# Mixing stage of a hybrid decoder layer: v with tokens on partitions, state products next to the first probabilities, SSM weights in room of their own, SSM outputs in token order

## The chip, the cores and the metric

The kernel runs on one core of a Trainium2 chip. The metric is the device time of one execution in microseconds (us); smaller is better. One execution was also recorded by the hardware profiler, which gives start and end of every instruction of TensorE (PE), its weight loads (PEld), VectorE (DVE), ScalarE (ACT), GpSimd (POOL) and of the DMA queues (SP issues nearly all transfers here).

## What is computed

One decoder layer over 512 tokens of width 1024: a first SwiGLU FFN, a mixing sub-layer, a second SwiGLU FFN, each between RMS norms, all in float32. The change is in the mixing sub-layer:

```python
h = rms_norm(x, mix_pre_g)
q, k, v, u = split(h @ w_mix_in, 4)              # four times 512 columns
attn = dilated_attention(q, k, v)                # 8 heads of 64; 3 dilations merged
ssm  = s5_mixer(u, ...)                          # 32 groups of 16 channels, 64 complex states
mixed = concatenate([attn, ssm], -1) @ w_mix_out
x = x + rms_norm(mixed, mix_post_g)
# s5_mixer: states by a linear recurrence over time; y = Re(C states) + d*u;
#           y = gelu(y); y * sigmoid(y @ w_glu + b_glu)
```

## The kernel before

**Number format.** Big products are made from three fp32r products each (high by high, high by low, low by high; `mm3`). So every weight tile is loaded raw (`load`, L99), cast to its high part on ACT (L93) and split off to its low part on DVE or POOL (L95). Raw tiles rotate through 3 buffers, the high and low parts through 4 each. Small products (scores, values, states, SSM outputs, transposes) are plain fp32; each fp32 product shows as two records.

**Layout.** Everything is held transposed: channels on partitions, the 512 tokens along the row. `mix` (from L835) runs in this order. Four u projections come ready from the boundary before. u is written to memory and read back in chunk order (a chunk is T = 4 tokens; 128 chunks, `U`). `proj` (from L844) makes a 128-channel piece of q, k or v: 24 products of 128x512, cut in two halves of 12 by a `yield`, and a DVE eviction (L856, L858) that also scales by the norm. A generator `pieces` lists the pieces; `f()` does the next half. v comes out with channels on partitions, and `turn_v` transposes it on PE (4 transposes for each head pair, L890) and copies it on ACT (L892).

**Attention.** For each of four head pairs: `attn_scores` (16 products; DVE adds the bias and takes the minimum, L793; ACT exponentiates, L795; the scaling by the sums is on DVE for pairs 0 and 1, on POOL and ACT for 2 and 3), `attn_turn` (10 transposes for each head, ACT copies L822), `attn_values` (16 products), `split` into the high and low halves of `cat`.

**SSM.** `states` (from L898) makes chunk states for 4 of 16 groups; `scan` (from L1058) runs the recurrence on DVE alone (L1064): 15 steps over the chunks of a row, one that copies, 6 over the row ends, and 4 that add the carried states. `go()` does one step. `outputs` (from L907) makes 4 groups' outputs from `M` (products of the last 4 inputs) and the states in `Hs`; its weights `w2` come by a DMA (L910) into a raw weight buffer. The outputs stand in the order (token within chunk, chunk); gelu follows on ACT and DVE, `glu` the gate, and the halves of `so` are written back in token order (L1046).

**Output projection.** `out_attn(m)` is the attention half: 12 products for each of 8 output tiles, with weights of 256 KB for each m. The SSM half (`yt`) is done in `boundary`, with the tail weights `tw` that `load_tail` has put in the pool `bdm`, which is opened where the attention pool `att` (scores, probabilities, q, k, v, and the scan's temporaries) was closed.

**What sets the order.** PE products and transposes, the projections' evictions and the scan's steps are pinned: each goes behind what was written before it for its engine (`fix`). Softmax, splits and weight loads are not pinned; a scheduler places them at build time by when their inputs and buffers are ready. Each engine then runs its queue strictly in order. PSUM has 8 banks.

Of the kernel before, what the change touches and what calls it, by code (L numbers as in the profile page):

```python
# [17 lines left out]
P = 128  # L18
S = 512
# [21 lines left out]
class Layer:  # L41
# [62 lines left out]
    def tail_weights(self, pool):  # L104

        self.tw = [pool.tile([P, KD * NT * P], F32R, name="tw", tag=f"tw{i}", bufs=1) for i in range(2)]

    def load_tail(self, src, c, pool):
        sl = slice(c * 2 * NT * P, (c + 1) * 2 * NT * P)
        self.load(src[c], (2 * NT, P), [t[:, sl] for t in self.tw], pool)  # L110
# [146 lines left out]
    def boundary(self, y, tail, ipost, half, inext, chunks):  # L257
# [4 lines left out]
        tw = [t.rearrange("p (m k j) -> p m k j", k=NT, j=P) for t in self.tw]  # L262
# [11 lines left out]
        def product(h, m):  # L274
            if m % 2 == 0 or m == 7:
                bank[0] = self.bank("yt").rearrange("p (m t) -> p m t", m=2)
            b = bank[0][:, m % 2 if m < 6 else 0]
            for k in range(NT):
                th, tl = tail(k)
                self.mm3(b, tw[0][:, m, k], tw[1][:, m, k], th[:, hs[h]], tl[:, hs[h]], k == 0, k == NT - 1)  # L280
            return bank[0]
# [32 lines left out]
        for ks in (range(NT - 1), (NT - 1,)):  # L314
            for m in range(2):
                for k in ks:
                    th, tl = tail(k)
                    self.mm3(b2[m], tw[0][:, m, k], tw[1][:, m, k], th[:, hs[0]], tl[:, hs[0]], k == 0, k == NT - 1)
# [52 lines left out]
    def ffn(self, n, first, scope, params):  # L371
# [68 lines left out]
        for f in range(NF):  # L440
            if f >= nfirst:
                products(f)
            if f == lag:
                for i in range(lag):
                    hidden(i)
            if f >= lag:
                hidden(f)
            if last and f == 6:
                for _ in hook:
                    pass  # L450
                yk = self.ktiles("y")
                y = lambda b, d: yk(2 * b + d)
            if last and f in (6, 12, 18):
                outp_tokens(f // 6 - 1)
            if not last and f in (7, 14):
                outp(f // 7 - 1)
            if f == NF - NT:
                for _ in hook:
                    pass
                early.close()  # L460
                self.tail_weights(scope.enter_context(self.tc.tile_pool(name="bd" + n, bufs=1)))
            if f >= NF - NT:
                self.load_tail(w_tail, f - (NF - NT), f % 2 == 1)
# [22 lines left out]
    def finish(self, y, tail):  # L486
# [3 lines left out]
        tw = [t.rearrange("p (k d c) -> p k d c", k=NT, d=2) for t in self.tw]  # L490
# [4 lines left out]
        def product(b, d, k0=0, k1=NT):  # L495
            if k0 == 0:
                o[b, d] = self.bank("yt")
            ts = slice(b * P, (b + 1) * P)
            for k in range(k0, k1):
                th, tl = tail(k)  # L500
                self.mm3(o[b, d], th[:, ts], tl[:, ts], tw[0][:, k, d], tw[1][:, k, d], k == 0, k == NT - 1)
# [323 lines left out]
    def attn_values(self, po, pt, vn):  # L825

        for kb in range(4):
            for i in range(2):
                self.mm(po[i * E:i * E + E, kb * P:], lhsT=vn[:, kb, i * E:i * E + E], rhs=pt[i][kb],
                        start=kb == 0, stop=kb == 3)  # L830
# [4 lines left out]
    def mix(self, first, scope):  # L835
        early = scope.enter_context(ExitStack())
# [49 lines left out]
        def turn_v(hp):  # L886

            o = self.bank("vt")
            for b in range(4):
                self.fix(nc.tensor.transpose(o[:, b * P:(b + 1) * P], pr[8 + hp][:, b * P:(b + 1) * P], self.ident))  # L890
            vn[hp] = ap.tile([P, 4, P], F32, name="vn", tag="vn", bufs=2)
            nc.scalar.copy(out=vn[hp].rearrange("p b c -> p (b c)"), in_=o)  # L892


        Hs = self.b16("Hs").rearrange("p (q n) (b k) -> p q (n b) k", q=2, k=NCH)
        ends = ap.tile([P, 2, NP, SC], F32, name="ends", tag="ends", bufs=1)
# [34 lines left out]
        mo = {}  # L931

        def out_attn(m, ks=range(4)):

            if m not in mo:
                mo[m] = self.bank("mo"), self.load(a["wmoa"][m], (4, P))
            o, (wh, wl) = mo[m]
            for k in ks:
                self.mm3(o, wh[:, k], wl[:, k], cat[:, k], cat[:, 4 + k], k == 0, k == 3)
# [9 lines left out]
        vn = {}  # L949
# [3 lines left out]
        def values(hp, pt):  # L953
            po = self.bank("pv")
            self.attn_values(po, pt, vn[hp])
            self.split(cat[:, hp], cat[:, 4 + hp], po)

        f()
        sc = scores(0)
        f(3)  # L960
        pt = [turn(sc[0])]
        f()
        pt.append(turn(sc[1]))
        f()
        sc = scores(1)
        states(0)
        states(4)
        turn_v(0)
        states(8)
        states(12)  # L970
        cat = self.b16("cat", F32R)
        scan = self.scan(ap, Hs, ends)
# [5 lines left out]
        def fg(n=1):  # L978
            for _ in range(n):
                f()  # L980
                go()

        values(0, pt)
        go(2)
        pt = [turn(sc[0])]
        fg()
        pt.append(turn(sc[1]))
        fg(5)
        for hp in (2, 3):
            sc = scores(hp)  # L990
            fg()
            turn_v(hp - 1)
            fg()
            values(hp - 1, pt)
            if hp == 2:
                go()
                pt = [turn(sc[0])]
                fg()
                pt.append(turn(sc[1]))
                fg(3)  # L1000
        go(7)
        pt = [turn(sc[0]), turn(sc[1])]
        y = self.ktiles("ymix")
        out_attn(0, range(3))
        go()
        turn_v(3)
        out_attn(1, range(3))
        values(3, pt)
        go()
        out_attn(2, range(3))  # L1010
        early.close()
        bdm = scope.enter_context(self.tc.tile_pool(name="bdm", bufs=1))
        self.tail_weights(bdm)
        zg = bdm.tile([P, 4, S], F32, name="zg")
        zt = self.b16("zz", F32R)
        tail = lambda c: self.load_tail(a["wmot"], c, False)
        for m in range(3):
            out_attn(m, (3,))
        go()
        out_attn(3)  # L1020
        for n4 in range(4):
            outputs(n4)
            if n4 < 3:
                if n4 == 0:
                    go()
                out_attn(4 + n4)
                tail(n4)
# [7 lines left out]
        def glu(m, ks=range(4)):  # L1035
# [4 lines left out]
            if 3 in ks:  # L1040
# [7 lines left out]
        for m in range(2):  # L1048
            glu(m, range(3))
        for m in range(2):  # L1050
            glu(m, (3,))
        glu(2)
        tail(3)
        glu(3)
        out_attn(7)
        return y, lambda i: (so[0][:, i], so[1][:, i])

    def scan(self, ap, Hs, ends):  # L1058
# [11 lines left out]
        def tmp(shape):  # L1070
            t = ap.tile([P, nb * (SI - 1) * SC], F32, name="sx", tag="scan", bufs=3)
# [26 lines left out]
        for n in range(0, NP, nb):  # L1098
# [12 lines left out]
            yield  # L1111
# [20 lines left out]
def pack(i):  # L1132
# [23 lines left out]
    o["wmi"] = mt(wm).reshape(16, P, D)  # L1156
    wo, o["wmot"] = two(mt(i["w_mix_out"][0]))
    o["wmoa"] = wo.reshape(KD, P, 4 * P)
# [34 lines left out]
```

## Time and profile before

| | us |
|---|---|
| median of 3 runs | 980.96 (978.39 to 981.84) |
| profiled execution, its time | 978.9 |
| its span, first to last instruction | 977.1 |
| PE busy | 948.4 |
| DVE, ACT, POOL busy | 532.9, 372.3, 223.5 |
| stage "mix" in the span | about 400 to 575 |

The time is the span and 1.8 us around it. The profile's page gives totals; for a stage of 175 us the useful views are the busy time in a stretch, the list of who waited for whom on PE, and the timeline of one engine, in which the idle time before an instruction and what ended it stand in brackets. A start-to-start distance in a timeline is what an instruction costs its engine; the duration printed beside it is longer, because the end of one overlaps the start of the next.

### The profile page before, as it was taken

The numbers are of one execution on the slowest core, as the hardware profiler recorded it, in microseconds if no ns is written. First come the engines' busy times: TensorE is split into PE (matmuls) and PEld (weight loads), VectorE is DVE, ScalarE is ACT, GpSimd is POOL, SyncE is SP. The second block draws the span as 40 slices with busy tenths as digits, with TensorE's granted clock in tenths as the row PEclk, the third lists the DMA queues.
The fourth block names the chain that finished last, engine by engine and source line by source line (L and its number), as shares of the span: only waits on it lengthen the run. The fifth ranks groups of instructions, "written<-read, shape, count | busy, mean of one in ns | idle before, by whom it ended". The sixth has DMA issues, their size and how long they took to land.

```text
span 977.1 us, 12902 instructions
## 1 busy us (share of the span) xinstructions
PE 948.4 (97%) x5088; PEld 792.6 (81%) x5088; DVE 532.9 (55%) x938; ACT 372.3 (38%) x616; POOL 223.5 (23%) x134
## 2 busy tenths in 40 slices
PE   9999999999999999999999699999999999999996
PEld 7888888888888899878667589888888888888884
DVE  7997214553265447658769567564225433444426
ACT  7353334431233234356553654443333222323312
POOL 2322212322233134300000024422122212222300
PEclk9999999999999999999999999999999999999998
DMA  8223334343343230473111530222223222333202
GB/s 261 91 103 113 103 119 150 100 166 103 108 131 116 76 130 23 118 211 120 54 51 50 185 126 23 92 95 93 89 87 108 101 93 87 108 98 131 95 0 87
DMA packets 38606, 102.48 MB, mean 105 GB/s; under 512 B 7665, under 2 KB 10737, under 8 KB 38001
## 3 DMA queue, kind: packets, MB, share of 16 engines
q1 hardware_dynamic: 37680, 98.50, 31.6%
q10 hardware_dynamic: 864, 3.15, 0.9%
q8 instruction: 40, 0.66, 0.3%
q14 instruction: 22, 0.17, 0.1%
HBM read 94.03 MB, written 7.60 MB: 104 GB/s over the span
## 4 chain that ended last, share of the span: by engine, by line
PE 86%; DVE 7%; ACT 3%; DMA 2%; issue 1%; POOL 0%; DVEq 0%; POOLq 0%; ACTq 0%
PE gu L121 46%; PE yo L121 20%; PE prj L121 6%; PE yt L121 5%; PE first L121 4%; PE st L121 1%; DVE sx L1064 1%; DVE Hs L1064 1%; DVE xl L144 1%; DMA wraw<-wmot 1%; DVE x L303 1%; PE pt L820 1%; ACT sc L795 1%; DMA w<-w2d 1%; PE idle L121 1%
## 5 line engine op out<-in xcount | busy, mean ns | idle before, releaser
L93 ACT CAST whi<-wraw 128x1024 fp32r<-128x1024 f32 (+5 forms) x161 | 155.8, 971 | 323.8 <-PE gu L121 126.9
L95 POOL TENSOR_TENSOR wlo<-wraw,whi 128x1024 fp32r<-128x1024 f32 (+2 forms) x62 | 156.3, 2521 | 525.9 <-ACT whi L93 525.9
L121 PE MATMUL gu<-xh,whi 128*128 128x512 f32 x656 | 257.6, 393 | 0.0
L121 PE MATMUL gu<-xh,wlo 128*128 128x512 f32 x656 | 255.6, 390 | 0.0
L121 PE MATMUL gu<-xl,whi 128*128 128x512 f32 x656 | 255.3, 389 | 0.0
L95 DVE TENSOR_TENSOR wlo<-wraw,whi 128x1024 fp32r<-128x1024 f32 (+5 forms) x99 | 111.6, 1130 | 124.9 <-ACT whi L93 124.5
L121 PEld LDWEIGHTS gu<-xh,wlo 128*128 128x128 f32 x656 | 123.1, 188 | 25.9
L121 PEld LDWEIGHTS gu<-xl,whi 128*128 128x128 f32 x656 | 123.2, 188 | 25.1
L121 PEld LDWEIGHTS gu<-xh,whi 128*128 128x128 f32 x656 | 123.2, 188 | 25.1 <-issue 0.4
L405 DVE TENSOR_TENSOR ut<-gu,rs 128x512 f32<-128x512 f32 x41 | 28.3, 689 | 104.0 <-PE gu L121 103.8
L141 DVE TENSOR_TENSOR al<-ut,ah 128x512 fp32r<-128x512 f32 x44 | 69.0, 1570 | 24.9 <-ACT ah L140 24.8
L121 PE MATMUL yo<-ah,whi 128*128 128x512 f32 x144 | 56.0, 389 | 0.0
L121 PE MATMUL yo<-al,whi 128*128 128x512 f32 x144 | 56.0, 389 | 0.0
L121 PE MATMUL yo<-ah,wlo 128*128 128x512 f32 x144 | 56.0, 389 | 0.0
L121 PE MATMUL yo<-whi,ah 128*128 128x512 f32 x144 | 56.0, 389 | 0.0
L121 PE MATMUL yo<-wlo,ah 128*128 128x512 f32 x144 | 56.0, 389 | 0.0
L121 PE MATMUL yo<-whi,al 128*128 128x512 f32 x144 | 56.0, 389 | 0.0
L403 DVE TENSOR_TENSOR gt<-gu,rs 128x512 f32<-128x512 f32 x41 | 28.2, 688 | 50.7 <-PE gu L121 50.6
L140 ACT CAST ah<-ut 128x512 fp32r<-128x512 f32 x44 | 27.2, 621 | 58.3 <-DVE ut L406 58.2
L121 PE MATMUL first<-xl,whi 128*128 128x256 f32 (+1 forms) x144 | 43.3, 300 | 2.2 <-DVE xl L144 2.2
L121 PE MATMUL first<-xh,whi 128*128 128x256 f32 (+1 forms) x144 | 43.9, 305 | 0.9 <-ACT xh L143 0.9
L406 DVE TENSOR_TENSOR ut<-ut,gt 128x512 f32<-128x512 f32 x44 | 40.7, 927 | 3.7
(192 smaller groups left out, 1426.9 us busy)
## 6 DMA issues: line engine op xcount, KB each, us to landing
wraw<-w2i SPq DMA_DIRECT2D x44, 512.0 KB, 3.5
wraw<-w1i SPq DMA_DIRECT2D x42, 512.0 KB, 3.5
wraw<-w2o SPq DMA_DIRECT2D x18, 512.0 KB, 3.5
wraw<-wmi SPq DMA_DIRECT2D x16, 512.0 KB, 3.5
wraw<-w1o SPq DMA_DIRECT2D x16, 448.0 KB, 3.4
x<-xT SPq DMA_DIRECT2D x8, 256.0 KB, 4.5
w1d<-w1s SPq DMA_DIRECT2D x8, 256.0 KB, 2.9
w2d<-zb SPq DMA_DIRECT2D x2, 1024.0 KB, 4.9
```

Of the source, the lines that this page charges most:

```text
L93: fix(self.nc.scalar.copy(out=hi, in_=raw))
L95: fix(eng.tensor_tensor(out=lo, in0=raw, in1=hi.bitcast(F32), op=ALU.subtract))
L121: i = self.nc.tensor.matmul(*a, **k)
L140: nc.scalar.copy(out=hi, in_=src)
L141: nc.vector.tensor_tensor(out=lo, in0=src, in1=hi.bitcast(F32), op=ALU.subtract)
L144: fix(nc.vector.scalar_tensor_tensor(out=lo, in0=src, scalar=scale, in1=hi.bitcast(F32), op0=ALU.mult, op1=ALU.subtract))
L303: fix(nc.vector.tensor_tensor(out=xk, in0=t, in1=xk, op=ALU.add))
L403: nc.vector.tensor_tensor(out=gt, in0=o[f][0], in1=r, op=ALU.mult)
L405: nc.vector.tensor_tensor(out=ut, in0=o[f][1], in1=r, op=ALU.mult)
L406: nc.vector.tensor_tensor(out=ut, in0=ut, in1=gt, op=ALU.mult)
L795: nc.scalar.activation(out=so, in_=so, func=AF.Exp, bias=nm[:, t:t + 1], scale=-1.0, accum_out=den[:, t:t + 1])
L1064: tt = lambda o, x, y, op: self.fix(V.tensor_tensor(out=o, in0=x, in1=y, op=op))
```

## The change

v is projected with tokens on partitions (`proj_v`: x is the stationary side, 512 columns of weights the moving side, evicted by ACT with the norm as a scale per partition), so `turn_v` goes. Both heads of pair 0 are turned and all `states` are made right after the first scores; all of v follows, in two pieces of 48 products. The scan has a pool of its own and starts its steps with v's pieces; its last four steps are cut in eight. `fg(i, ...)` does, for each i, `f()` and then `go(i)`. The low half of `cat` is pinned behind a step of the scan. `out_attn` takes its weights for two m at a time (512 KB) and is split up finer. The four `w2` loads get tiles in `bdm` (in the room that the last tail weights take later) and are issued together when `att` is closed. The four `outputs` come back to back and write PSUM with a stride, so that they stand in token order; `so` is then written straight. Tail weights are eight tiles in place of two.

```diff
-            t = pr[c] = ap.tile([P, S], F32, name="qkvT"[c // 4] + "T", tag="qk", bufs=5)
+            t = pr[c] = ap.tile([P, S], F32, name="qkT"[c // 4] + "T", tag="qk", bufs=4)
...
+        def proj_v(b0):
+            o = [self.bank("prv") for _ in range(2)]
+            for k in range(KD):
+                wh, wl = wv[k // 2]
+                for b in range(2):
+                    ts = slice((b0 + b) * P, (b0 + b + 1) * P)
+                    self.mm3(o[b], xh(k)[:, ts], xl(k)[:, ts], wh[:, k % 2], wl[:, k % 2], k == 0, k == KD - 1)
+                if k % 2:
+                    if k == KD - 1:
+                        for b in range(2):
+                            nc.scalar.activation(out=vn[:, b0 + b], in_=o[b], func=AF.Copy,
+                                                 scale=r4[:, b0 + b:b0 + b + 1])
+                    yield
...
-            w2 = self.wp.tile([P, 2, 4, P], F32, name="w2", tag="wraw", bufs=3)
-            nc.sync.dma_start(out=w2, in_=self.w2d[:, :, 4 * n4:4 * n4 + 4])
+            w2 = w2s[n4]
             b = self.bank("ys")
+            bt = b.rearrange("p (s i t) -> p t i s", s=SC, t=T)
...
-                        o = b[n * 32:(n + 1) * 32, t * NCH:(t + 1) * NCH]
+                        o = bt[n * 32:(n + 1) * 32, t]
...
-            for c in (1, 5, 8, 2, 6, 9, 3, 7, 10, 11):
+            for c in (1, 5):
+                yield from proj(c)
+            wv.extend(self.load(a["wmv"][k2], (2, S)) for k2 in range(4))
+            for b in (0, 2):
+                yield from proj_v(b)
+            for c in (2, 6, 3, 7):
                 yield from proj(c)
...
+            nc.scalar.copy(out=cat[:, hp], in_=po)
+            return lambda: self.fix(nc.vector.tensor_tensor(out=cat[:, 4 + hp], in0=po, in1=cat[:, hp].bitcast(F32),
+                                                            op=ALU.subtract))
...
+        pt = [turn(sc[0]), turn(sc[1])]
+        for n4 in range(0, NP, 4):
+            states(n4)
...
+        fg(1, 1, 1, 2)
+        sc = scores(1)
+        fg(1, 1, 1, 1)
+        low = values(0, pt)
+        go()
+        low()
+        fg(1)
+        pt = [turn(sc[0])]
+        fg(1)
+        pt.append(turn(sc[1]))
+        fg(1, 1)
+        low = values(1, pt)
+        go()
+        low()
+        sc = scores(2)
+        fg(1, 1, 2, 2)
+        pt = [turn(sc[0]), turn(sc[1])]
+        sc = scores(3)
+        y = self.ktiles("ymix")
+        go(2)
+        out_attn(0, (0, 1))
+        out_attn(1, (0, 1))
+        low = values(2, pt)
+        go(2)
+        low()
+        out_attn(2, (0, 1))
+        go()
+        for m in range(3):
+            out_attn(m, (2,))
         pt = [turn(sc[0]), turn(sc[1])]
         go()
+        out_attn(3, range(3))
+        low = values(3, pt)
         early.close()
         bdm = scope.enter_context(self.tc.tile_pool(name="bdm", bufs=1))
+        w2s = [bdm.tile([P, 2, 4, P], F32, name="w2", tag=f"tw{3 - n // 2}{n % 2}", bufs=1) for n in range(4)]
+        for n in range(4):
+            self.dma(out=w2s[n], in_=self.w2d[:, :, 4 * n:4 * n + 4])
...
+        out_attn(4, range(3))
+        go()
+        low()
+        for m in range(5):
             out_attn(m, (3,))
+            if m % 2:
+                go()
+        go(9)
         for n4 in range(4):
             outputs(n4)
+        for c in range(2):
+            tail(c)
...
-                v = lambda w: w.rearrange("p (s i j) -> p j i s", j=T, s=SC)
-                self.split(v(so[0][:, m]), v(so[1][:, m]), t2.rearrange("p (j i s) -> p j i s", j=T, s=SC))
+                self.split(so[0][:, m], so[1][:, m], t2)
...
+        for m in range(4):
             glu(m, range(3))
+        for c in range(2, 4):
+            tail(c)
+        for m in range(4):
             glu(m, (3,))
+        for m in range(5, KD):
+            out_attn(m)
```

## Rows read from the trace of the kernel before

**Rows 1.** The page's first part, over the whole span: busy time, share, instructions of each engine.

```profile
PE 948.4 (97%) x5088; PEld 792.6 (81%) x5088; DVE 532.9 (55%) x938; ACT 372.3 (38%) x616; POOL 223.5 (23%) x134
```

**Rows 2.** Busy time of each engine in the mixing stage (columns: stretch, its length, then PE, PEld, DVE, ACT, POOL busy, granted clock, DMA share, GB/s).

```profile
400.00:575.00 175.00, 160.44 (x1173) 126.59 (x1173) 123.20 (x293) 92.08 (x193) 12.46 (x10) 0.99 0.40 121
```

**Rows 3.** Who PE waited for between 400 and 580 us (us in total, times, longest).

```profile
PE ys L121 <- DMA w<-w2d: 5.6, 2, 3.1
PE pv L121 <- ACT vn L892: 4.1, 2, 2.1
PE yt L121 <- DVE so L141: 1.4, 2, 0.7
PE mo L121 <- DVE cat L141: 1.4, 1, 1.4
PE gl L121 <- ACT zz L140: 0.9, 1, 0.9
PE gl L121 <- DVE zz L141: 0.8, 1, 0.8
```

**Rows 4.** The same columns as Rows 2, for a stretch of the SSM outputs in which the granted clock is lower.

```profile
550.30:554.00 3.70, 3.67 (x80) 3.44 (x84) 1.29 (x2) 1.57 (x2) 0.00 (x0) 0.57 0.23 91
```

**Rows 5.** Timeline of PE (start, us, engine, line, operation, shape, count, idle before): the first probabilities' turn, the first SSM outputs and what follows them, and the start of the SSM half of the output projection.

```profile
430.70 1.25 PE L820 MATMUL pt<-ident,sc 128*128 128x128 f32 x10
...
526.95 0.42 PE L121 MATMUL ys<-um 128*32 128x128 f32 x8
...
529.71 0.73 PE L121 MATMUL mo<-cat,whi 128*128 128x512 f32 x2
...
570.41 1.26 PE L121 MATMUL yt<-so,tw 128*128 128x256 f32 x7
572.39 1.58 PE L121 MATMUL yt<-so,tw 128*128 128x256 f32 x11 [0.72 <-DVE so L141]
...
575.28 4.93 PE L121 MATMUL yt<-so,tw 128*128 128x256 f32 x39 [0.72 <-DVE so L141]
```

**Rows 6.** Pieces of the chain of work that ended last, in order of time (start, us, engine, what, count): scores, transposes of v, states, values, turns, projections.

```profile
438.58 2.36 PE sc L121 x16
...
444.71 0.44 PE vt L890 x4
445.15 3.57 PE st L121 x32
448.72 2.30 PE pv L121 x16
...
455.02 1.09 PE pt L820 x10
456.12 13.66 PE prj L121 x60
```

**Rows 7.** The copy of v on ACT after its transposes, from the groups of ACT's instructions between 395 and 580 us (busy, mean ns | idle before).

```profile
L892 ACT COPY vn<-vt 128x512 f32<-128x512 f32 x4 | 2.3, 586 | 1.2 <-PE vt L890 1.2
```

**Rows 8.** Timeline of DVE: softmax of pair 1 (first minimum, the first split after the eighth, the scaling of one head), the low half of `cat` for pair 0, the first operations of two steps of the scan, of two steps over the row ends, and of two halves of a last step.

```profile
439.67 0.69 DVE L793 CUSTOM_DVE_ANT_0 sc<-sc,bias 128x512 f32<-128x512 f32 x1 [0.32 <-PE sc L121]
...
442.96 1.22 DVE L95 TENSOR_TENSOR wlo<-wraw,whi 128x1024 fp32r<-128x1024 f32 x1
...
445.30 1.27 DVE L804 TENSOR_SCALAR sc<-sc,rd 128x128 f32<-128x128 f32 x4
...
451.69 0.69 DVE L141 TENSOR_TENSOR cat<-pv,cat 128x512 fp32r<-128x512 f32 x1 [0.67 <-ACT cat L140]
452.30 0.75 DVE L1064 TENSOR_TENSOR sx<-pw,Hs 128x256 f32<-128x256 f32 x2
...
453.95 0.76 DVE L1064 TENSOR_TENSOR sx<-pw,Hs 128x256 f32<-128x256 f32 x2
...
511.75 0.34 DVE L1064 TENSOR_TENSOR sx<-pw,Hs 128x32 f32<-128x32 f32 x2
...
512.56 0.34 DVE L1064 TENSOR_TENSOR sx<-pw,Hs 128x32 f32<-128x32 f32 x2
...
514.93 1.23 DVE L1064 TENSOR_TENSOR sx<-pw,Hs 128x480 f32<-128x480 f32 x2
...
517.33 1.22 DVE L1064 TENSOR_TENSOR sx<-pw,Hs 128x480 f32<-128x480 f32 x2
```

**Rows 9.** Busy time of DVE from the first operation of the scan to its last (stretch, length, DVE busy, granted clock, DMA share, GB/s).

```profile
452.30:535.90 83.60, 66.47 (x192) 1.00 0.16 50
```

**Rows 10.** Timeline of all engines, around the room for the tail weights: issue of the first tail load (SP), last operation of the scan (DVE), first cast into the new room (ACT).

```profile
510.45 0.33 SPq L99 DMA_DIRECT2D wraw<-wmot  x1
...
535.25 0.65 DVE L1064 TENSOR_TENSOR Hs<-Hs,sx 128x480 f32<-128x480 f32 x1
...
535.98 1.05 ACT L93 CAST tw<-wraw 128x1024 fp32r<-128x1024 f32 x1 [1.37 <-DVE Hs L1064]
```

**Rows 11.** The page's row for the `w2` loads (count, KB each, median us from issue to landing).

```profile
w<-w2d SPq DMA_DIRECT2D x4, 512.0 KB, 5.3
```

**Rows 12.** The halves of `so`, written with a stride of 64 elements (durations ns min/median/max, first and last start).

```profile
L140 ACT CAST so<-go x4: 1126/1138/1164, 564.9 to 573.0; 128x512 fp32r<-128x512 f32 x4
L141 DVE TENSOR_TENSOR so<-go,so x4: 1071/1081/2391, 566.1 to 574.1; 128x512 fp32r<-128x512 f32 x4
```

**Rows 13.** The like cast on ACT written straight, from the groups of ACT's instructions between 395 and 580 us (busy, mean ns | idle before).

```profile
L140 ACT CAST zz<-zg 128x512 fp32r<-128x512 f32 x4 | 2.5, 617 | 0.9 <-DVE zg L927 0.9
```

More of the change, by code (lines that the diff above doesn't have):

```diff
@@ L102, in load, with load_tail @@
         return v(hi), v(lo)
[L104 to L110, printed above, removed]
+    def load_tail(self, tp, src, c, pool):
+        if c == 0:
+            self.tw = []
+        self.tw.append([tp.tile([P, 2 * NT * P], F32R, name="tw", tag=f"tw{c}{i}", bufs=1) for i in range(2)])
+        self.load(src[c], (2 * NT, P), self.tw[c], pool)
     def fix(self, i):
@@ L261, in boundary @@
         w = [self.load(c, (KD, P), pool=i % 2 == 1) for i, c in enumerate(chunks)]
-        tw = [t.rearrange("p (m k j) -> p m k j", k=NT, j=P) for t in self.tw]
+        tw = lambda i, m, k: self.tw[m // 2][i].rearrange("p (m k j) -> p m k j", k=NT, j=P)[:, m % 2, k]
         hs = [slice(0, HT), slice(HT, S)]
@@ L489, in finish @@
         nc, V, fx = self.nc, self.nc.vector, self.fix
-        tw = [t.rearrange("p (k d c) -> p k d c", k=NT, d=2) for t in self.tw]
+        tw = lambda i, k, d: self.tw[k][i][:, d * S:(d + 1) * S]
         sums = self.sp.tile([P, 4, 2], F32, name="sums", tag="sums")
@@ L835, in mix @@
     def mix(self, first, scope):
+        sx = scope.enter_context(self.tc.tile_pool(name="scan", bufs=2))
         early = scope.enter_context(ExitStack())
@@ L884, in mix @@
             pass
[L886 to L892, printed above, removed]
         Hs = self.b16("Hs").rearrange("p (q n) (b k) -> p q (n b) k", q=2, k=NCH)
-        ends = ap.tile([P, 2, NP, SC], F32, name="ends", tag="ends", bufs=1)
+        ends = sx.tile([P, 2, NP, SC], F32, name="ends", tag="ends", bufs=1)
         def states(n4):
@@ L929, in outputs @@
             nc.scalar.mul(z, z, 0.25)
-        mo = {}
+        mo, wm = {}, {}
         def out_attn(m, ks=range(4)):
+            if m // 2 not in wm:
+                wm[m // 2] = self.load(a["wmoa"][m // 2], (8, P))
             if m not in mo:
-                mo[m] = self.bank("mo"), self.load(a["wmoa"][m], (4, P))
-            o, (wh, wl) = mo[m]
+                mo[m] = self.bank("mo")
+            o, (wh, wl) = mo[m], wm[m // 2]
             for k in ks:
-                self.mm3(o, wh[:, k], wl[:, k], cat[:, k], cat[:, 4 + k], k == 0, k == 3)
+                i = 4 * (m % 2) + k
+                self.mm3(o, wh[:, i], wl[:, i], cat[:, k], cat[:, 4 + k], k == 0, k == 3)
             if 3 in ks:
@@ L954, in values @@
             po = self.bank("pv")
-            self.attn_values(po, pt, vn[hp])
-            self.split(cat[:, hp], cat[:, 4 + hp], po)
+            self.attn_values(po, pt, vn, hp)
+            nc.scalar.copy(out=cat[:, hp], in_=po)
+            return lambda: self.fix(nc.vector.tensor_tensor(out=cat[:, 4 + hp], in0=po, in1=cat[:, hp].bitcast(F32),
+                                                            op=ALU.subtract))
         f()
         sc = scores(0)
+        vn = ap.tile([P, 4, S], F32, name="vn", tag="vn", bufs=1)
         f(3)
[L961 to L970, printed above, removed]
+        pt = [turn(sc[0]), turn(sc[1])]
+        for n4 in range(0, NP, 4):
+            states(n4)
         cat = self.b16("cat", F32R)
-        scan = self.scan(ap, Hs, ends)
+        scan = self.scan(sx, Hs, ends)
         def go(n=1):
@@ L976, in go @@
                 next(scan, None)
-        def fg(n=1):
-            for _ in range(n):
-                f()
-                go()
-        values(0, pt)
-        go(2)
[L985 to L1000, printed above, removed]
@@ L1001, in mix, with fg @@
-        go(7)
+        def fg(*n):
+            for i in n:
+                f()
+                go(i)
+        fg(1, 1, 1, 2)
[16 more added lines that the diff above has]
+        sc = scores(3)
@@ L1002, in mix @@
+        y = self.ktiles("ymix")
+        go(2)
+        out_attn(0, (0, 1))
[7 more added lines that the diff above has]
+            out_attn(m, (2,))
         pt = [turn(sc[0]), turn(sc[1])]
-        y = self.ktiles("ymix")
-        out_attn(0, range(3))
-        go()
[L1006 to L1010, printed above, removed]
+        go()
@@ L1017, in mix @@
-        for m in range(3):
+        tail = lambda c: self.load_tail(bdm, a["wmot"], c, False)
+        out_attn(4, range(3))
+        go()
+        low()
+        for m in range(5):
             out_attn(m, (3,))
-        go()
-        out_attn(3)
+            if m % 2:
+                go()
+        go(9)
         for n4 in range(4):
             outputs(n4)
[L1023 to L1027, printed above, removed]
+        for c in range(2):
+            tail(c)
@@ L1044, in glu, with scan @@
                 nc.vector.scalar_tensor_tensor(out=t2, in0=t, scalar=1.0, in1=zg[:, m], op0=ALU.add, op1=ALU.mult)
-                v = lambda w: w.rearrange("p (s i j) -> p j i s", j=T, s=SC)
-                self.split(v(so[0][:, m]), v(so[1][:, m]), t2.rearrange("p (j i s) -> p j i s", j=T, s=SC))
-        for m in range(2):
+                self.split(so[0][:, m], so[1][:, m], t2)
+        for m in range(4):
             glu(m, range(3))
-        for m in range(2):
+        for c in range(2, 4):
+            tail(c)
+        for m in range(4):
             glu(m, (3,))
[L1052 to L1055, printed above, removed]
+        for m in range(5, KD):
+            out_attn(m)
         return y, lambda i: (so[0][:, i], so[1][:, i])
-    def scan(self, ap, Hs, ends):
+    def scan(self, sx, Hs, ends):
         V = self.nc.vector
@@ L1070, in tmp @@
         def tmp(shape):
-            t = ap.tile([P, nb * (SI - 1) * SC], F32, name="sx", tag="scan", bufs=3)
+            t = sx.tile([P, nb * (SI - 1) * SC], F32, name="sx", tag="scan", bufs=2)
             n = math.prod(shape)
@@ L1110, in scan @@
                 tt(d[:, q], d[:, q], t2, SUB if q == 0 else ADD)
-            yield
+                yield
     def run(self, parts="fmg"):
```

21 lines of the change are left out of this document (10 added, 11 removed).

## The prediction

> **What bounds the kernel now.** I read the page first: over the whole span PE is busy 97% [rows 1], so only work taken from PE, or time in which PE stands still, can be won. Then busy time by stretch, to find where it stands still: in the mixing stage it is busy 160.4 of 175 us [rows 2]. The list of PE's waits names the 14.2 us: 5.6 for the `w2` loads, 4.1 for v's copy on ACT, 2.8 for the two halves of `so` and the last half of `cat`, 1.7 for the halves of `zz` [rows 3]. Last the clock: after the two `w2` waits the granted clock is 0.57 from 550.3 to 554, nearer to the lower of its two levels, 1.2 GHz, than to 2.4 [rows 4]. There 80 records of the SSM outputs take 3.67 us; the first outputs' 96 took 529.71 - 526.95 = 2.76 us [rows 5], so 80 should take 2.3, and 1.4 us are lost.
>
> **The frame of the sum.** Both kernels are alike up to the first turn of probabilities at 430.70. The SSM half of the output projection runs without a stop from 575.28; 18 of its products ran before, worth 18 x 4.93/39 = 2.3 us [rows 5]. So it stands at an undisturbed start of 573.0, and the old path is 142.3 us.
>
> **PE work of the new path,** start to start. Products of 512 columns: 13.66/60 = 0.228 us each [rows 6]; v 96 (as many as before, operands swapped), the other q and k pieces 96, attention half of the output 96, gate 48: 336 x 0.228 = 76.5. Turns 8 x 1.09 = 8.7, scores 3 x 2.36 = 7.1, values 4 x 2.30 = 9.2, states 64 records at 3.57/32 = 7.1 [rows 6]. SSM outputs 4 x 2.76 = 11.0 if the stride costs PE nothing (below). Sum 119.6: without any wait the start would be 550.3, or 22.7 us earlier. That holds the 16 transposes of v (4 x 0.44 = 1.8 us [rows 6]), the 14.2 of waits, the 1.4 of clock, and some 5 us in which matmuls drain ahead of each wait and which the records count as busy. What comes back:
>
> (a) *v's copy* no longer sits behind the exponentials, but `values(0)` follows the last piece of v at once and needs two copies on ACT of 0.586 us [rows 7]: 1.2 and a drain of 0.2, so 1.4 us. Bounds: 0.6, if one of the two is done by then, and the old worst wait of 2.1 [rows 3].
>
> (b) *The scan moves ahead of PE's need, and DVE becomes what PE waits for.* `low()` of pair 2 is pinned behind the 25th of the scan's 30 steps, and the third products of three output tiles need it. DVE's list up to there: 15 steps at 453.95 - 452.30 = 1.65, 24.8; the copying step 0.4; 6 at 512.56 - 511.75 = 0.81, 4.9; three half steps at 517.33 - 514.93 = 2.40, 7.2; minima of three pairs at 442.96 - 439.67 = 3.3, 9.9; scaling of pair 1, 2 x 1.27 and its reciprocals 0.3, 2.8; seven splits of 1.2, 8.4; four evictions and three low halves at 452.30 - 451.69 = 0.61, 4.3 [rows 8]. Sum 62.7 us. It begins when the states are evicted and v's fourth weight tile is split (the first step is pinned behind that split): PE ends the states at 430.70 + 2.2 + 7.1 = 440.0, so about 442.5. Idle time on top: DVE was idle 17.1 of 83.6 us while the scan ran [rows 9], mostly before evictions pinned ahead of a step; v's pieces have no eviction on DVE now, four q and k pieces still do and pair 1's scaling waits for ACT. I take 6 us, so `low()` is done at 442.5 + 62.7 + 6 = 511.2. PE gets there after six turns 6.5, states 7.1, 192 products of v, q and k 43.8, three scores 7.1, three values 6.9, 18 products of the output 4.1, together 75.5 us, and (a): at 507.6. So a wait of 3.6 us. Bounds: nothing, if DVE is idle under 2.5 us; 13.2 if it stays idle in the old proportion (62.7 x 83.6/66.5 = 78.9). I take the low side, since the evictions are fewer.
>
> (c) *Gate.* The first gate tile needs groups 0 to 2 of the SSM outputs, and only group 3's 2.76 us and six gate products (1.4) lie between the end of group 2 and the third of them. The chain behind a group is six operations on ACT and DVE in turn, some 0.6 each as the cast in rows 13 and the evictions in rows 8, plus the hand-overs: 4 to 5 us. I take 0.8, half of the old 1.7 [rows 3]; bounds 0 and 1.7. At the end of the stage 36 products (8.2 us) now lie between the last gate product and its use, longer than that chain, so the 1.6 us for `so` go and nothing comes back.
>
> (d) *`w2`.* The four loads are issued when `att` is given back, behind the last `values`. The trace shows that a new pool waits for the closed one: the first tail load was issued at 510.45, its cast began at 535.98, right after the scan's last operation at 535.25 + 0.65 [rows 10]. PE has 24 products, 5.5 us, before the first outputs; a `w2` load took 5.3 us [rows 11], and later ones have 2.76 us more each. I take 0; the rest of `w2`'s risk is a rival. Loads queued behind them on SP are tail and gate weights, due 10 us later. Nothing moves on POOL.
>
> (e) *Clock.* After (b)'s wait I expect a stretch at the lower level as after the old waits: 1.2 of the 1.4 us there [rows 4]; bounds 0 and 2.8.
>
> Drains at three waits: 0.9. Back come 1.4 + 3.6 + 0.8 + 1.2 + 0.9 = 7.9 us, so 22.7 - 7.9 = 14.8 are saved: 978.9 - 14.8 = 964.1 against the profiled execution (span 977.1 and 1.8 around it). That one lies 2.1 under the median of the runs, 980.96; as a median I forecast **966**.
>
> **Rival 1: strided PSUM writes slow the SSM outputs.** No row shows PE writing with a stride. The nearest rows are ACT and DVE writing `so` with one, in SBUF: 1.138 us on ACT against 0.617 straight [rows 12, 13], x1.84, and on DVE 1.075 against 0.69 [rows 8, 12], x1.56. Below nothing it cannot go. On 11.0 us of outputs, now with nothing beside them on PE, that is 6.2 to 9.3 us: 972 to 975. Against it: each output product is fp32 and takes two records, four products run side by side, and a record takes about 4 x 2.76/96 = 0.115 us for 128 columns, half the rate of the fp32r products (0.228 us for 512), so the write side has slack. The Trainium skill speaks for it ("PSUM — Partial Sum Buffer", Specifications (TRN2)): PSUM has 8-byte cachelines, and any non-contiguous pattern slows matmuls significantly. By that rule a halved write rate would double the outputs, which is an estimate of 977; no trace here shows it. Chance 0.26.
>
> **Rival 2: the wait for `w2` only moves.** If the weights of `out_attn(4)` are queued on SP behind the four `w2` loads, PE stands right after the last `values` for issue, transfer and split. A load takes 5.3 us [rows 11], a cast 1.05 and a split 1.2 [rows 8, 10]: 7.6 us if it runs beside the four, 12.9 if it starts when they have landed, so 974 to 979. For it: SP runs in order, and the `w2` loads are pinned. Against it: that weight load isn't pinned, and loads ran far ahead before (the tail load at 510.45 [rows 10]). Chance 0.09.
>
> **Rival 3, slower: the stride costs PE far more than ACT.** The same 384 records; it decides from x2.6 on (966 + 1.6 x 11.0 = 983.6, the edge of what can be told). At x4, 999. For it speaks only that accumulation reads each element back; against it that no strided writer here loses more than x1.84 [rows 12, 13]. Chance 0.09.
>
> **How the numbers follow.** Forecast 0.56 (960 to 975, the bounds of (b) and (e) carrying nearly all of it), rivals 0.26, 0.09, 0.09. A measurement of this kernel tells about 0.3%, 2.9 us, from no change: under 978.0 is faster, over 983.9 slower. Faster: 0.55 of the forecast, 0.23 and 0.04 of rivals 1 and 2, 0.82; same 0.08; slower 0.10. The range runs from 959 (no wait for DVE, no clock loss, and the runs' own spread of 2) to 979 (the tops of rivals 1 and 2, with the spread of 2 on rival 1 again), and leaves out rival 3 and a little of the rest.
>
> **What would show it.** Right: no waits for `w2` or for v's copy behind exponentials; the states ahead of 441; PE's longest wait in the stage before a third product of `out_attn`, released by the low half of `cat`; DVE near 90% busy from 442 to 511; a record of SSM outputs still 0.029 us apart; `so` at about 0.6 and 0.7 us. Wrong: outputs of 4.3 us or more per group (rival 1 or 3); a wait for weights after the last `values` (rival 2); a DVE wait of 8 us or more, which means that pinned steps hold it up more than I took.

## The result, and the profile after

The changed kernel takes **973.87 us** (median of 6 runs, 969.98 to 976.56), the kernel before 981.66 in the same series: ratio 0.9921, 95% interval 0.9903 to 0.9938. It is 7.8 us faster, about half of what was forecast. The profiled execution ran 973.89 us (span 972.1).

Busy time of the mixing stage, as in [rows 2] (columns as there). The second stretch is the one in which the scan now runs, the last one the gate:

```profile
400.00:575.00 175.00, 165.98 (x1195) 132.42 (x1196) 121.90 (x288) 91.75 (x192) 16.11 (x13) 0.96 0.43 131
441.00:512.00 71.00, 68.03 (x347) 50.44 (x345) 59.08 (x189) 38.78 (x94) 4.64 (x4) 1.00 0.27 89
512.00:560.00 48.00, 42.71 (x509) 33.60 (x510) 30.25 (x45) 23.50 (x40) 0.00 (x0) 0.86 0.36 122
...
548.00:552.00 4.00, 3.71 (x9) 2.69 (x9) 2.56 (x4) 1.87 (x4) 0.00 (x0) 0.50 0.38 131
```

PE's busy time in the 175 us rose from 160.4 to 166.0, but the granted clock fell from 0.99 to 0.96, all of it behind 512 (1.00 from 400 to 512): at 548 to 552 it is 0.50, the lower of the two levels. Busy time at half the clock is not work done, so the two columns must be read together. Whom PE waited for between 400 and 580 us, as in [rows 3]:

```profile
PE mo L120 <- ACT cat L973: 3.1, 1, 3.1
PE gl L120 <- ACT zz L139: 1.7, 1, 1.7
PE sc L120 <- ACT ptt L821: 1.1, 1, 1.1
PE ys L120 <- issue: 0.9, 1, 0.9
PE mo L120 <- DVE cat L974: 0.8, 1, 0.8
...
PE gl L120 <- DVE zz L140: 0.5, 2, 0.3
```

The waits for `w2` (5.6), for v's copy (4.1) and for `so` are gone. The longest now stands at a third product of `out_attn`, the place that was forecast; but what ends it is the high half from ACT, and the low half only adds 0.8. On the timeline of PE, the rows that answer to [rows 5]:

```profile
431.57 2.34 PE L819 MATMUL pt<-ident,sc 128*128 128x128 f32 x20
...
531.09 0.43 PE L120 MATMUL ys<-um 128*32 128x128 f32 x8
...
533.73 0.40 PE L120 MATMUL ys<-um 128*32 128x128 f32 x8
...
568.39 15.99 PE L120 MATMUL yt<-so,tw 128*128 128x256 f32 x132
```

The new path is 568.39 - 431.57 = 136.8 us, against 142.3 before and 127.5 forecast (573.0 - 14.8 = 558.2, less 430.7). So of the 22.7 us taken out, 136.8 - 119.6 = 17.2 came back, not 7.9. A group of SSM outputs takes 533.73 - 531.09 = 2.64 us.

**The gate.** From the first of its 48 products to the first product behind them it takes 560.23 - 542.91 = 17.3 us, where 48 x 0.228 = 10.9 [rows 6] is their work:

```profile
542.91 0.74 PE L120 MATMUL gl<-zz,whi 128*128 128x512 f32 x2
...
560.23 0.62 PE L120 MATMUL mo<-cat,whi 128*128 128x512 f32 x2
```

The chain of work that ended last, in order of time (start, us, what), says why:

```profile
531.97 1.15 DVE tw L95
533.13 6.26 DMA wraw<-wmot
539.41 1.05 ACT tw L93
540.46 0.52 ACT zz L139
...
543.49 0.58 ACT ge L932
544.07 0.93 ACT tw L93
545.01 0.53 ACT zz L139
...
548.64 11.75 PE gl L120 x41
```

A tail weight, not needed before 568, is on the path of a gate product at 545: its cast stands in ACT's queue ahead of a gelu operation, and its load was issued only at 533.13, when the split at 531.97 had freed a raw buffer, behind the four `w2` loads. The wait of 1.1 us at the scores of pair 3 has the same form: ACT stands for the load of a gate weight, ahead of the copies (L821) that the scores wait for:

```profile
499.70 1.04 ACT L93 CAST whi<-wraw 128x1024 fp32r<-128x1024 f32 x1 [2.64 <-DMA wraw<-wgl]
```

**The low half of pair 2.** Timeline of all engines:

```profile
509.05 3.73 ACT L805 ACTIVATE sc<-sc,rd 128x128 f32<-128x128 f32 x8 [0.94 <-POOL rd L799]
...
512.69 0.56 ACT L973 CAST cat<-pv 128x512 fp32r<-128x512 f32 x1
512.86 1.34 DVE L1085 TENSOR_TENSOR Hs<-Hs,sx 128x480 f32<-128x480 f32 x2
...
513.30 0.80 PE L120 MATMUL mo<-cat,whi 128*128 128x512 f32 x1 [3.14 <-ACT cat L973]
514.13 0.68 DVE L974 TENSOR_TENSOR cat<-pv,cat 128x512 fp32r<-128x512 f32 x1
...
514.87 0.79 PE L120 MATMUL mo<-cat,whi 128*128 128x512 f32 x1 [0.77 <-DVE cat L974]
```

The low half starts at 514.1 and is done at 514.7 (forecast 511.2); on DVE there is no gap ahead of it. But the first to be late is the high half on ACT, behind eight scalings of softmax 3. The clock then stays low for some 6 us (0.72 from 508 to 520). Busy time from the first scan step to the start of the low half (columns as in [rows 2]), and the splits among DVE's groups in that stretch (busy, mean ns | idle before):

```profile
442.00:514.13 72.13, 67.82 (x343) 49.90 (x342) 60.27 (x193) 39.03 (x93) 4.64 (x4) 0.99 0.26 85
...
L95 DVE TENSOR_TENSOR wlo<-wraw,whi 128x1024 fp32r<-128x1024 f32 x9 | 11.0, 1222 | 5.4 <-ACT whi L93 5.4
```

### The profile page after: what moved, and what is told of

Read it like the earlier page. It is cut to its first block, busy times and chain, and to the rows that moved or that the text cites. A ratio compares the mean times of both kernels' runs of the same rounds, so it can differ in the third digit from the quotient of the medians.

```text
span 972.1 us, 12842 instructions
## 1 busy us (share of the span) xinstructions
PE 949.6 (98%) x5072; PEld 793.7 (82%) x5072; DVE 528.9 (54%) x930; ACT 370.9 (38%) x612; POOL 223.3 (23%) x134
## 4 chain that ended last, share of the span: by engine, by line
PE 88%; DVE 6%; ACT 2%; DMA 2%; issue 1%; SPq 0%; POOL 0%; DVEq 0%; POOLq 0%; ACTq 0%
PE gu L120 46%; PE yo L120 20%; PE yt L120 6%; PE first L120 3%; PE prj L120 3%; PE prv L120 2%; PE mo L120 1%; PE st L120 1%; PE gl L120 1%; DVE xl L143 1%; DVE x L302 1%; PE pv L120 1%; PE pt L819 1%; DVE Hs L1085 1%; DMA wraw<-wmot 1%
## 5 line engine op out<-in xcount | busy, mean ns | idle before, releaser
L120 PE MATMUL first<-xh,wlo 128*128 128x256 f32 (+1 forms) x144 | 42.4, 295 | 0.0
```

The costliest lines, as they stand in the source:

```text
L120: i = self.nc.tensor.matmul(*a, **k)
```

## The experiments

Theory **T1**: casts of weights that come late stand in the in-order queues of ACT and DVE and stop PE, at the scores of pair 3 and at the gate. Rivals: **R2**, outputs back to back leave the gelu chain too little time; **R3**, the burst of four `w2` loads does it directly. For the wait at pair 2, theory **C** was formed during the runs: two holds of the same length, ACT's queue and DVE's pinned scan. Of the parts of the change itself, only the stride and the room for `w2` were undone by themselves; how the 7.8 us divide among the others is not shown. Ratios are to the kernel before, measured in the same series; "path" is from the first turn of probabilities to an undisturbed start of the SSM half, taken as above (where its first products ran ahead of a stop, 2.3 us are taken off for them as in the prediction).

**Gate loads first.** The program lines of the first two tail loads moved behind the first gate products; this turns the order of the loads and leaves the casts of the late tails ahead of gelu operations:

```
-        for c in range(2):
-            tail(c)
...
-        for c in range(2, 4):
+        for c in range(4):
             tail(c)
```

> The changed kernel (973.87 median) with one thing moved: the two loads of gate weights are issued ahead of the first two loads of tail weights, so that the tails no longer hold two of three raw buffers while the gate weights queue for the third. Theory T1 (late weights, whose casts stand in the in-order queues of ACT and DVE, stop PE): the wait of 1.13 us at the scores of pair 3 and DVE's idle 1.53 us ahead of a gate-weight split go; the gate's waits (1.69 + 0.23 + 0.29) and the low granted clock after them stay, since the third tail's cast still stands ahead of the gelu operations: 971 to 973. Rival R2 (the copies of the probabilities are late by themselves; the gelu chain is too long for the distance given to it): neither moves, 973.5 to 974.5.

Measured: 972.41 us, 0.9907 (0.9890 to 0.9925), path 134.9. The wait at the scores is gone from the list; the gate's waits stand (2.1 and 0.7). This half of T1 holds in the trace; as a time its 1.5 us lies within the intervals of both kernels.

**Casts of the tails behind the gelu operations.** The loads of the gate weights are written ahead of the outputs, which gives the order of loads as above, and the tails' load, cast and split are pinned where they are written, behind the last group of outputs (`load` hands `fix` on to all three; the tails of the other stages stay unpinned):

```
-        self.load(src[c], (2 * NT, P), self.tw[c], pool)
+        self.load(src[c], (2 * NT, P), self.tw[c], pool, (lambda i: i) if pool is not None else self.fix)
```

> As x1_gate_loads_first, and the casts and splits of all four tail weights are pinned on ACT and DVE behind the gelu operations of the last group of SSM outputs. The four w2 loads stay where they are, in one burst. T1: the gate waits under 0.5 us in all, the granted clock over the gate is 0.95 or more, its 48 products take 11 to 12 us in place of 17.3, and the SSM half of the output projection runs from 561 to 563: 966 to 969. R2 (outputs back to back leave the gelu chain too little time): a wait of 1 to 2 us for zz stays, and the low clock behind it: 971 to 973. R3 (the burst of w2 loads starves PE or the queues directly): as R2, 971 to 973, with the pause of 0.9 us in the outputs still there.

Measured: 971.8 us, 0.9899 (0.9880 to 0.9919), path 134.5. Whom PE waited for between 400 and 580 us:

```profile
PE mo L120 <- ACT cat L973: 3.5, 1, 3.5
PE ys L120 <- issue: 1.4, 1, 1.4
PE mo L120 <- ACT whi L93: 1.1, 1, 1.1
PE mo L120 <- DVE cat L974: 1.1, 1, 1.1
PE mo L120 <- DVE wlo L95: 0.9, 1, 0.9
```

No wait for `zz` is left, and the gate's 48 products take 554.46 - 543.41 = 11.1 us, with outputs back to back and the `w2` burst in place: R3 falls for the gate, and R2 as the cause of its 6 us. (PE stops here for 1.4 us in the outputs, which gives the gelu chain that much more time; what is left of R2 without such a stop shows further down.) The time missed the forecast because the last weights of `out_attn` were now late (1.1 + 0.9 at 558 to 560, with a clock of 0.66 from 560 to 565).

**That mended.** Those weights are loaded and cast ahead of the tails:

```
+        wm[3] = self.load(a["wmoa"][3], (8, P), fix=self.fix)
         for c in range(2):
             tail(c)
```

> x2_gate_first_tails_last (971.8) with its new wait mended: there the last weights of the attention half of the output were loaded last of all, and PE stood 1.07 + 0.91 us for their cast and split at 558 to 560, with a clock of 0.66 behind it. Here they are loaded and cast ahead of the four tail weights, still behind the gelu operations. T1: this wait and its clock go, no wait stands from the first output product to the SSM half of the output projection, which starts 130 to 131 us after the first turn (x2 134.5): 967.5 to 969.5. If the late tail weights take its place (the third and fourth tail), a wait for tw appears inside yt: 970 to 972.

Measured: **967.81 us**, 0.9862 (0.9841 to 0.9883), path 130.9. The gate and what follows, in one stretch:

```profile
542.00:556.00 14.00, 14.00 (x87) 11.23 (x77) 8.62 (x11) 9.88 (x15) 0.00 (x0) 1.00 0.26 92
```

PE is busy without a gap at full clock. T1 is worth 6.1 us, though no work was taken away and the same bytes are loaded.

**The scan left out.** All multiplies and adds of the recurrence are left out, so the states are not carried on (likewise the steps over the row ends and the last half steps):

```
-            step(ends if i == SI - 1 else h[:, :, :, i + 1], ...)
```

> The changed kernel without the arithmetic of the scan (all multiplies and adds of the state recurrence are left out on DVE, only the two operations that write the first column stay), so that DVE is light from 442 to 525. Theory T2 (DVE's pinned scan steps make PE wait for the low half of cat of pair 2, and hold up the minima of pair 3, whose scaling on ACT stands ahead of the high half): both waits there (3.14 + 0.77) go with the low clock behind them, some 5 to 6 us: 966 to 970, the gate's waits staying. Rival T2b (ACT's own load or the reciprocals on POOL set it): a wait of 2 us or more for the high half stays, 971 to 974.

Measured: 968.1 us, 0.9869 (0.9847 to 0.9891), path 131.6. The time came as expected of T2, the wait did not:

```profile
PE mo L120 <- ACT cat L973: 2.4, 1, 2.4
PE ys L120 <- issue: 2.3, 2, 2.0
PE sc L120 <- ACT ptt L821: 1.3, 1, 1.3
...
PE gl L120 <- DVE zz L140: 0.6, 1, 0.6
PE mo L120 <- DVE cat L974: 0.2, 1, 0.2
```

With DVE nearly empty, 2.4 of 3.1 us stay with ACT. A total that fits does not show the mechanism; the gain lay at the gate, whose 48 products took 555.92 - 543.61 = 12.3 us in place of 17.3 (waits of 0.8 in place of 2.2, clock 1.00 from 544 to 552). Hence theory C, and three edits.

**The high half first on ACT.** The reciprocals and scalings of softmax 3 are written behind `values(2)`, whose cast is pinned (`late_scale` holds them until then):

```
         low = values(2, pt)
+        for s in late_scale:
+            s()
         go(2)
         low()
```

> The changed kernel (973.87 median) with one thing moved on ACT: the cast that makes the high half of cat for pair 2 stands ahead of the eight scalings of softmax 3 (with their reciprocals on POOL), not behind them; it can then run at about 508.5 in place of 512.69. x3_no_scan showed that ACT's own queue holds this half back even without the scan. Theory C (two holds of the same length: ACT's queue until 513.3, and the two scan steps pinned on DVE ahead of the low half until 514.8): the wait only changes its name, about 4 us for DVE's low half in one piece or two, 973 to 974.5. Rival A (ACT's order alone): the wait falls to 1 us or less and the low clock behind it goes, 969 to 971.

**The low half first on DVE.**

```
         low = values(2, pt)
-        go(2)
         low()
+        go(2)
```

> The changed kernel with one thing moved on DVE: the low half of cat for pair 2 is pinned ahead of the two scan steps that stood ahead of it; ACT's order is as it was at this place. Theory C: DVE now stands until ACT's high half is made at 513.3, so the wait for the high half (3.1 us) stays and only the 0.77 behind it goes: 972.5 to 974. Rival B, the prediction's reading (the pinned scan alone): both go, with the low clock, 968 to 970.

**Both.**

> x5 and x6 together. Theory C: the low half is ready about 510, the wait of 3.9 us falls below 1 us, the granted clock after it stays near 1.0; the turns of pair 3, whose scaling is done at about 513.5, then wait 0.5 to 1.5 us, since 6 products (1.4 us) lie between: 969 to 971. If the gain of the two together is that of the larger one alone (no lock in common), C falls.

Measured: 972.94 us, 0.9916 (0.9889 to 0.9942); 971.7, 0.9897 (0.9873 to 0.9921); both together **968.46**, 0.9864 (0.9842 to 0.9885). Paths 137.7, 137.5, 130.4. The first alone:

```profile
509.46 0.59 ACT L976 CAST cat<-pv 128x512 fp32r<-128x512 f32 x1 [0.52 <-PE pv L120]
...
515.69 0.79 PE L120 MATMUL mo<-cat,whi 128*128 128x512 f32 x1 [4.46 <-DVE cat L977]
```

The second alone:

```profile
512.58 0.69 DVE L974 TENSOR_TENSOR cat<-pv,cat 128x512 fp32r<-128x512 f32 x1 [3.88 <-ACT cat L973]
512.60 1.52 PE L120 MATMUL mo<-cat,whi 128*128 128x512 f32 x2 [3.13 <-ACT cat L973]
```

Both, PE's stretch from 508 to 520:

```profile
508.00:520.00 12.00, 12.00 (x75) 8.73 (x72) 11.83 (x21) 8.00 (x21) 2.50 (x2) 1.00 0.00 1
```

Each alone only changes the name of the wait; together they end it and its clock loss. The times lie 0.1 to 0.8 us under the ranges of theory C (that of the second alone still above rival B's), so it is these rows that decide for C. The expected wait of the turns for their scaling did not come; 2.4 us for the low half of pair 3 did.

**All of it, and the low half of pair 3 ahead of its scan step.**

```
         out_attn(4, range(3))
-        go()
         low()
+        go()
```

> x8_gate_clear and x7_both_halves_first together: gate weights loaded ahead of the tails, the tails' casts behind the gelu operations, and both halves of cat for pair 2 ahead of the scalings and of the scan steps. If the two causes (weight casts in the queues, and the two holds on the halves of pair 2) are separate, their gains add up: 973.87 - 6.1 - 5.4 = 962.4, less what x7 already had back in the gate (about 1): 962 to 965. A wait for the low half of pair 3 (2.4 us in x7) may stay, shorter by the split of tail weights that stood ahead of it. If both only shift the same later wait, 966 to 968.

> x9_all_mended with the low half of cat for pair 3 pinned ahead of the scan step that stood ahead of it. By theory C the wait for that half (1 to 2.4 us) goes: 961 to 963.5. If the wait goes and the state products of the third or fourth group then wait for the last scan step, the same as x9 or 1 us more.

Measured: 964.37 us, 0.9817 (0.9792 to 0.9841), path 124.8, with 1.4 us for the low half of pair 3; without that wait **960.42**, 0.9787 (0.9764 to 0.9809), path 123.4. So the two causes are separate and add up: in the path 5.9 and 6.4 us alone, 12.0 together. Of the 4 us between the last two medians the path shows only 1.4; in the profiled executions 1.4 more lie ahead of the first turn and 1.5 behind the stage, where the edit changes nothing. The last one, waits and the stage:

```profile
PE gl L120 <- ACT zz L139: 1.2, 1, 1.2
...
PE gl L120 <- DVE zz L140: 0.2, 1, 0.2
PE yt L120 <- DVE so L140: 0.2, 1, 0.2
...
400.00:575.00 175.00, 173.05 (x1311) 142.73 (x1312) 127.25 (x301) 95.93 (x198) 19.30 (x15) 1.00 0.42 130
```

This is what is left of R2: 1.2 + 0.2 us for `zz` (0.4 + 0.2 in the version before it), though no cast of weights stands among the gelu operations any more. The chains of the groups follow one another on ACT and DVE 535.53 - 532.17 = 3.36 us apart, while PE makes a group in 2.64:

```profile
532.17 0.69 DVE L140 TENSOR_TENSOR zz<-zg,zz 128x512 fp32r<-128x512 f32 x1 [0.69 <-ACT zz L139]
...
535.53 0.69 DVE L140 TENSOR_TENSOR zz<-zg,zz 128x512 fp32r<-128x512 f32 x1 [0.68 <-ACT zz L139]
```

With the gate cleared in the changed kernel alone, PE's stop of 1.4 or 1.0 us in the outputs hid this.

**Outputs straight again, and token order alone.** The first undoes the stride in the changed kernel, the second puts it alone into the kernel before; the halves of `so` change with it:

```
-                        o = bt[n * 32:(n + 1) * 32, t]
+                        o = b[n * 32:(n + 1) * 32, t * NCH:(t + 1) * NCH]
```

> The changed kernel with the SSM outputs written straight into PSUM again (a step's chunks side by side) and the two halves of so written with the stride of 64 elements again. If the stride in PSUM costs PE nothing (2.64 us for a group of 96 records, as read): a group stays at 2.6 to 2.75 us, so takes 1.14 and 1.08 us in place of 0.62 and 0.69, and of this at most 1 us reaches PE since 36 products lie between: 973.5 to 975.5. Rival 1 of the prediction (strided writes slow the outputs): a group falls to 1.4 to 1.7 us, 970 to 972.

> The kernel before with one part alone of the change: SSM outputs written into PSUM in token order (stride of 4 elements), and the halves of so straight. All instructions stand in the same order on every engine. If the stride is free: 96 records of outputs take 2.64 to 2.76 us as before, casts of so 0.62 and 0.69 us in place of 1.14 and 1.08, and the waits for so (1.4 + 0.2 us) fall below 0.5: 1 to 2.5 us faster than the kernel before. By rival 1 of the prediction: outputs 4.3 us or more for 96 records, 4 to 8 us slower.

Measured: 972.57 us, 0.9910 (0.9890 to 0.9930), a group of outputs 535.35 - 532.70 = 2.65 us as against 2.64 strided, the cast of `so` 1.158 us as against 0.622, with no wait for `so` either way; and 979.98, 0.9985 (0.9966 to 1.0004), where the waits for `so` fell from 1.4 + 0.2 to 0.6. The first time lies between the two ranges, so the group of outputs decides: the stride costs PE nothing. It is not a stride of 4 elements, as was written before the second run: along a product's 128 columns the view `bt` runs over s first, so neighbouring columns lie 64 elements apart in PSUM, eight in a row, and each next row starts 4 elements on. That is the order in which the halves of `so` were written in SBUF. What the order in PSUM saves on ACT and DVE is real only where PE waits for `so`, and there it is too small for this measurement.

**`w2` through the raw buffers again.**

```
-            w2 = w2s[n4]
+            w2 = self.wp.tile([P, 2, 4, P], F32, name="w2", tag="wraw", bufs=3)
+            nc.sync.dma_start(out=w2, in_=self.w2d[:, :, 4 * n4:4 * n4 + 4])
```

> The changed kernel with one part undone: the four w2 loads go through the three raw buffers again, so that the loads of gate and tail weights queue behind them. If w2's own room is worth what the prediction took (5.6 us of waits and 1.4 of clock), a wait for w2 of the later groups or for the gate weights behind them comes back on PE: 976 to 982. If the order of the rest (outputs back to back, loads far ahead) hides them now, 972.5 to 975.

Measured: 972.63 us, 0.9908 (0.9884 to 0.9931). Waits:

```profile
PE gl L120 <- ACT whi L93: 5.1, 1, 5.1
PE mo L120 <- ACT cat L974: 2.4, 1, 2.4
PE mo L120 <- DVE cat L975: 1.1, 1, 1.1
```

The time lies in the range for loads that are hidden, but the rows say something else: no wait for `w2`, but 5.1 us for the gate weights, which now queue for the raw buffers; the waits for `zz` and at the scores are gone. Room of its own for `w2` gained nothing by itself: it traded this wait for the blocked gelu chain.

## Why the prediction was right and wrong

- **The frame held.** With the waits cleared the path is 123.4 us, with 1.6 of waits in it; 119.6 was forecast for the work alone. Waits for `w2`, v's copy and `so` went as forecast, and no rival came: outputs stay at 2.64 us a group (rivals 1 and 3), no wait for weights follows the last `values` (rival 2). The rule of the Trainium skill ("PSUM — Partial Sum Buffer", Specifications (TRN2)) that any non-contiguous pattern slows matmuls significantly is not borne out for these fp32 outputs of 128 columns with a stride of 64 elements.
- **(a)** 1.4 forecast, nothing measured: `values(0)` began right behind v's last piece (its record starts 0.31 us after v's last one); the two copies on ACT started at 464.86, before v's last record at 465.06.
- **(b)** 3.6 forecast, 3.1 + 0.8 measured: the cause was half of it, and the size came out right in part by luck, since both ends of the difference came late by more than the first turn (0.87): PE was there at 513.30 - 3.14 = 510.2 (forecast 507.6), the low half done at 514.7 (forecast 511.2). DVE's work up to its start was 60.3 us, no more than the 62.7 summed, although nine splits stood in it and not seven; its idle time was 72.1 - 60.3 = 11.9 us and not 6, of which 5.4 ahead of splits whose cast on ACT was late. DVE was 57.2 / 69 = 83% busy from 442 to 511, not near 90%. And ACT, which was not listed at all, held the high half until 513.3. Taking away what the prediction named would have left most of the wait, as the runs without the scan and with the low half first showed.
- **(c) is the step that failed**, with the sentence in (d) that led to it: "Loads queued behind them on SP are tail and gate weights, due 10 us later." The use is due then, the cast is not: it is an instruction in ACT's queue, and everything behind it waits for the load. The gate took 17.3 us in place of 10.9 + 0.8; 2.2 of it are listed as waits, the rest are drains and products 0.43 us apart at the lower clock. The same thing cost 1.1 us at the scores of pair 3, where the prediction had no term. Clearing both paid 6.1 us. The mechanism that (c) did name, a gelu chain too long for its distance, is there too, with 1.4 us in the last version; (c) priced the chain of one group and left out that the chains queue behind one another.
- **(e)** 1.2 forecast for one stretch at the lower clock; there are two (0.72 from 508 to 520, 0.50 from 548 to 552), each behind a wait. They cost some 2 us each: from 514.87, 8 products took 3.6 us in place of 1.8, from 548.64, 10 took 4.4 in place of 2.3.
- In us: 17.2 came back. T1's part is 136.8 - 130.9 = 5.9, C's part 130.9 - 124.8 = 6.1, the low half of pair 3 1.4 (124.8 - 123.4; it is no wait in the changed kernel and shows only once C's are cleared), and 3.8 are left (1.6 listed waits, the rest not taken apart). Forecast were 0.8, about 5 ((b) with (e)), nothing, and 2.3.
- Slips in the sums that change nothing: the upper bound in (b) is 442.5 + 78.9 - 507.6 = 13.8, not 13.2; 19 products of the SSM half ran ahead of 575.28, not 18 (one more at 574.17), and 4.93 is a printed duration: at 0.116 us start to start they give 573.1 for 573.0.
- The profiled spans differ by less (977.1 and 972.1) than the medians, as the prediction allowed for: the profiled execution of before lies 2.1 under its median.

## What to carry to other kernels

Cost a moved or delayed load by every instruction that waits for it, and by what stands behind that instruction on its in-order engine, not by when the data is used. Before a wait is put down to one engine, look for a second one that is late to the same point: with two holds of one length each edit alone shows nothing, and both must be tried together. After a gain, read the granted clock beside the busy time: 2.2 us of waits cost some 4 more behind them here.

## What the runs showed of the hardware that was not expected

- PE writes fp32 products into PSUM with a stride of 64 elements at the same rate as straight (2.64 and 2.65 us for 96 records), while ACT and DVE lose x1.86 and x1.64 on a stride of 64 elements in SBUF (1.158 and 0.622, 1.122 and 0.684 us, medians of `so`).
- Executions of one and the same program differ by 6.6 us (969.98 to 976.56), and their mean granted clock goes with it (0.995 and 0.993 at 970, 0.99 at 974, 0.988 and 0.986 at 976.5). The last version, with 1.6 us of waits in the stage, lies within 2 us (959.99 to 962.00, clock 0.995 to 0.997).
- In the SSM outputs PE stops for 0.2 to 2.0 us in most of the changed versions with nothing in the profile that it waits for (0.9 up to 538.62 in the changed kernel), and not at all in the kernel before and in the two fastest versions. Where it is 1.4, up to 539.12, the DMA engines are idle in the last microsecond (share 0.00 from 538 to 539). What the records do show: one DMA queue carries instructions, in packets of 16 KB, and in all twelve such stops (ten versions) PE goes on 2.3 to 2.5 us after the start of one of these packets. In the changed kernel that packet starts at 536.1 (first line, of the DMA queues from 536 to 537: packets, MB, share):

```profile
q8 instruction: 1, 0.02, 6.7%
...
538.62 0.31 PE L120 MATMUL ys<-Hs,w 128*32 128x128 f32 x4 [0.91 <-issue]
```

So PE may stand there for its own instructions. The profile does not say which engine a packet is for, and no run tests it: the cause stays open.
